# Sample retention states of a hybrid S5/retention step: vector multiply-adds with broadcast values in place of matmuls on split operands

## The chip, the cores and the metric

The kernel runs on one core of one Trainium2 chip. The metric is the device time of one execution in microseconds; lower is better. A core has five engines that run at the same time, each with its own instruction stream: TensorE (PE: matmuls and transposes, results in PSUM), VectorE (DVE), ScalarE (ACT), GpSimd (POOL) and SyncE (SP), whose queue here issues nearly all DMAs. On-chip data lies in SBUF, with 128 partitions, and in PSUM.

## The reference

One inference step of a single decoder layer, for a prompt of 256 positions and for 8 sample sequences of 8 positions each, 320 tokens together. RMS norm, one input projection to an S5 part and to q, k, v and gate of 8 retention heads of width 128, output projection, then a SwiGLU FFN (2048 to 5632 and back) and a last norm. The part that the change touches is the new retention state of the samples:

```python
gamma_h = 1 - 2 ** (-5 - h)                      # h = 0..7
# chunk of l = 8 positions for the samples, one state r0 (128 x 128) per head and sequence
k_decay = gamma_h ** (7 - t)                     # t = 0..7
r_new   = r0 * gamma_h ** 8 + einsum('md,me->de', k * k_decay[:, None], v)
```

So each of 64 states is the old one, scaled, plus eight outer products of a key with a value. The states are only an output; nothing later in the step reads them. Prompt states, attention outputs and the S5 part are as usual for such layers.

## The kernel before

All 320 tokens are columns of every matmul: columns 0 to 255 the prompt, 256 to 319 the samples (8 sequences b of 8 positions t). Every weight matrix is read once, in blocks of 128 x 1024 (512 KB, eight 128 x 128 tiles). To keep fp32 accuracy with the faster fp32r matmul, each operand is split in two parts: `wload` loads a block as `raw` (SP), ACT casts it to `hi` (L131), DVE subtracts to get `lo` (L133), and `gemm` runs three matmuls for each 128 x 128 tile: hi by hi, hi by lo, lo by hi (L143 to L145). In the first stages the pool `wp` holds three buffers each of raw, hi and lo; from the second FFN product on, a pool `wp2` with 4, 3 and 3 takes its place for weights, and `wp` is free for other use.

Stages in order of time: the input projection, one 128-wide column block after another (0 to 350 us of the span), and between its matmuls the S5 chunks and the retention heads; then output projection and GLU (350 to 485 us); then the FFN (to 1425 us), in four parts: `ffn_in(c)` makes 11 of 44 column pairs (gate, up), `ffn_out(c)` multiplies them by their part of the second matrix, in the order in 0, in 1, out 0, in 2, out 1, in 3, out 2, out 3.

What sets the order: PE and POOL run in the order in which the program traces them (a manual schedule). A small planner (`clk`, `spawn`, `run_due`) sums estimated matmul costs and resumes generators when their due time has come; so `head_k` runs 8.5 planned us after the k projection of its head, `head_v` 6.1 us after that of v. On DVE, ACT and SP a scheduler fixes the order at compile time from priorities; `wload` has a high one, so weights run ahead, and `tc.issue_after(x)` puts instructions behind x on x's engine.

The steps around the change:

- `do_k(h)`, after the k projection: `rot` makes the rotated keys `k_` (ACT, DVE), then POOL copies the sample columns to half of `ksp` (L883). `ksp` and `qsp` collect two heads.
- `head_k(h)`: PE transposes `k_` in three pieces into `pst` (L107), ACT scales two of them to `kd` for the prompt (L728) and the third to `kv[64:128, h]` (L729), the decayed keys of the samples by row. Then `pss`: scores of the prompt, and for odd heads `ksp` by `qsp`, the scores of two heads' samples. DVE multiplies by masks (`sm`, `smp`).
- `head_v(h)`: transposes of v, ACT scales them to `vT`, and copies the sample rows to `vsp` (L756) and to `kv[0:64, h]` (L757).
- The states, in `ffn_in(0)`: `states_split` splits `kv` into hi and lo and spreads both over partitions with 16 DMAs on ACT's queue; `states_load(h)` loads the eight old states of a head as `rt` (tag raw) and makes `vm`, the values masked per sequence (`bmk`); `states_add(h)` runs two matmuls of 512 columns into `psu` and two DVE instructions that scale the old states and add, then stores:

```python
ps = norm_ps("psu")
pe.matmul(ps, SU["k"][i][:, h], vm[:, q].rearrange("p b e -> p (b e)"), start=True, stop=True)
stt(rt[:, q], rt[:, q], float(GAM[h] ** NS), ps.rearrange("p (b e) -> p b e", e=P), MUL, ADD)
```

Of the kernel before, what the change touches and what calls it, by code (L numbers as in the profile page):

```python
# [12 lines left out]
F32 = mybir.dt.float32  # L13
F32R = mybir.dt.float32r
# [3 lines left out]
ADD, SUB, MUL = ALU.add, ALU.subtract, ALU.mult  # L18
PSUM = bass.MemoryType.PSUM

P = 128
D = 2048
KT = D // P
NP, NB, NS = 256, 8, 8
N = NP + NB * NS
H = 8
# [16 lines left out]

@with_exitstack
def hybrid_kernel(ctx, tc, xT, w_in, w_in4, w_out, w_glu, w_fi, w_fo, vecs, s5p, bc, x0,
                  r0, trig, masks, kdec, bmask, gq,
                  yT, s5p_o, s5s_o, rp_o, rs_o):
    nc = tc.nc
    pe, act, dve, pool, sp = nc.tensor, nc.scalar, nc.vector, nc.gpsimd, nc.sync
# [5 lines left out]
    def f(t):  # L55
        return t.bitcast(F32)
# [6 lines left out]
    mhalf = cst.tile([P, 4], F32, name="mhalf")  # L63
    pool.memset(mhalf, -0.5)
    vec = cst.tile([P, vecs.shape[1]], F32, name="vec")
    bmk = cst.tile([P, 4], F32, name="bmk")

    kv = cst.tile([P, H, P], F32, name="kv")
    voff = {}
    o = 0  # L70
    for nm, n in (("g_mix", 16), ("g_ffn", 16), ("g_fin", 16), ("d", 8), ("bglu", 8), ("gn", 8)):
# [33 lines left out]
    def tr(out, in_):  # L105
        m = in_.shape[0]
        pe.transpose(out, in_, ident[:m, :m])  # L107
        clk.now += 0.12
# [8 lines left out]


    wpool = [wp, (3, 3, 3)]
    last_hi = [None]  # L120

    def wload(src, nk, offset=3000):

        out = []
        with tc.high_priority(offset=offset):
            for k0 in range(0, nk, 8):
                m = min(8, nk - k0)
                raw, hi, lo = (wpool[0].tile([P, 8, P], d, name=n, tag=n, bufs=wpool[1][i])
                               for i, (n, d) in enumerate((("raw", F32), ("hi", F32R), ("lo", F32R))))
                sp.dma_start(raw[:, :m], src[:, k0:k0 + m])  # L130
                cast = act.copy(hi[:, :m], raw[:, :m])  # L131
                last_hi[0] = cast
                dve.tensor_tensor(lo[:, :m], raw[:, :m], f(hi[:, :m]), SUB)  # L133
                out += [(hi[:, i], lo[:, i]) for i in range(m)]
        return out

# [40 lines left out]
    def tt(out, a, b, op):  # L177
        dve.tensor_tensor(out, a, b, op)  # L178
        return out

    def stt(out, a, s, b, o1, o2):
        dve.scalar_tensor_tensor(out, a, s, b, o1, o2)
        return out
# [64 lines left out]
    rbc = mp.tile([P, N], F32, name="rbc")  # L248
    rtok = mp.tile([P, 3], F32, name="rtok")
    csr = mp.tile([P, 2, N], F32, name="csr")  # L250
    kdc = mp.tile([P, H, 3], F32, name="kdc")
    gqt = mp.tile([P, H, NS], F32, name="gqt")
    retp = mp.tile([P, H, N], F32, name="retp")

# [450 lines left out]
    def rot(ps, name):  # L705
        assert rot_t["ready"]
        with tc.high_priority(offset=EVAC):
            return rot_(ps, name)
# [11 lines left out]
    def head_k(h, q_, qg, k_, R):  # L720
        yield DL["k"]
        pst = misc("pst")
        for i, s in enumerate(STARTS):
            tr(pst[:, P * i:P * i + P], k_[:, s:s + P])
        kd = mp.tile([P, 2, P], F32, name="kd", tag="kd", bufs=1)
        with tc.high_priority(offset=EVAC):
            for i in range(2):
                act.mul(kd[:, i], pst[:, P * i:P * i + P], kdc[:, h, i:i + 1])  # L728
            act.mul(kv[64:128, h], pst[64:128, 2 * P:3 * P], kdc[64:128, h, 2:3])  # L729
        pss = misc("pss")  # L730
        mm(0.43, pss[:, 0:256], k_[:, 0:P], q_[:, 0:256], start=True, stop=True)
        mm(0.22, pss[:, 256:384], k_[:, P:256], q_[:, P:256], start=True, stop=True)
        if h % 2:
            mm(0.22, pss[:, 384:512], ksp, qsp, start=True, stop=True)
        sm = mp.tile([P, 384], F32, name="sm", tag="sm", bufs=1)
        mk = R["mk"]
        with tc.high_priority(offset=EVAC):
            tt(sm[:, 0:256], pss[:, 0:256], mk[:, 0:NP], MUL)
            last = dve.tensor_tensor(sm[:, 256:384], pss[:, 256:384], mk[:, 0:P], MUL)
            if h % 2:  # L740
                tt(smp, pss[:, 384:512], mk[:, NP:NP + P], MUL)
        if h == 0:
            with tc.issue_after(last.ins):
                s5_params3()
        R["kd"], R["sm"] = kd, sm

    def head_v(h, v_, qg, rt, R):
# [5 lines left out]
        with tc.high_priority(offset=EVAC):  # L753
            for i in range(3):
                act.mul(vT[:, i], pst2[:, P * i:P * i + P], rtok[:, i:i + 1])
        act.copy(vsp[64 * (h % 2):64 * (h % 2) + 64], vT[64:128, 2])  # L756
        last = act.copy(kv[0:64, h], vT[64:128, 2])  # L757
        if h == 0:
            rot_t["values"] = last
            with tc.issue_after(last.ins):  # L760
# [118 lines left out]
    def do_k(h, ps=None):  # L879
        ps = proj(9 + 4 * h) if ps is None else ps  # L880
        R = HS[h]
        k_ = rot(ps, "k_")
        pool.tensor_copy(ksp[:, 64 * (h % 2):64 * (h % 2) + 64], k_[:, NP:N])  # L883
        spawn(head_k(h, R["q_"], R["qg"], k_, R))
        run_due()
# [71 lines left out]
        k0 = k1  # L957
    ps0, ps1, pq, pk = accs
    for t_, s_ in ((x0t, x0), (csr, trig), (kdc, kdec),
                   (bmk, bmask), (gqt, gq)):  # L960
        sp.dma_start(t_, s_)
    for c in range(2):
        load_bc(c)
# [169 lines left out]
    def norm_ps(name):  # L1133
        return ps_n.tile([P, 512], F32, name=name, tag="n", bufs=2)
# [7 lines left out]

    SU = {}

    def states_split():
        kvh, kvl = (wp.tile([P, 8, P], F32R, name=n, tag=n, bufs=3) for n in ("hi", "lo"))
        act.copy(kvh, kv)
        tt(kvl, kv, f(kvh), SUB)  # L1150
        SU["k"] = [wp.tile([P, 8, P], F32R, name="hi", tag="hi", bufs=3) for _ in range(2)]
        SU["v"] = [wp.tile([P, 8, P], F32R, name="lo", tag="lo", bufs=3) for _ in range(2)]
        for i in range(2):
            for a in range(4):
                d = slice(32 * a, 32 * a + 32)
                act.dma_start(f(SU["k"][i][d]), f((kvh, kvl)[a // 2][64 + 32 * i:96 + 32 * i]))
                act.dma_start(f(SU["v"][i][d]), f((kvh, kvl)[a % 2][32 * i:32 * i + 32]))

    def states_load(h):
        rt = wp.tile([P, NB, P], F32, name="raw", tag="raw", bufs=3)  # L1160
        sp.dma_start(rt, r0[h])
        n = ("hi", "lo")[h % 2]
        vm = wp.tile([P, NB, P], F32R, name=n, tag=n, bufs=3)
        with tc.high_priority(offset=EVAC):
            for i in range(2):
                tt(vm[:, 4 * i:4 * i + 4], f(SU["v"][i][:, h]).unsqueeze(1).to_broadcast([P, 4, P]),
                   bmk.unsqueeze(2).to_broadcast([P, 4, P]), MUL)
        SU[h] = rt, vm

    def states_add(h):  # L1170
        rt, vm = SU.pop(h)
        for i in range(2):
            q = slice(4 * i, 4 * i + 4)
            ps = norm_ps("psu")
            pe.matmul(ps, SU["k"][i][:, h], vm[:, q].rearrange("p b e -> p (b e)"), start=True, stop=True)
            stt(rt[:, q], rt[:, q], float(GAM[h] ** NS), ps.rearrange("p (b e) -> p b e", e=P), MUL, ADD)
        sp.dma_start(rs_o[h], rt)

    def ffn_in(c):
        ahi = fp.tile([P, FCT, N], F32R, name="ahi", tag="ahi", bufs=2)  # L1180
        alo = fp.tile([P, FCT, N], F32R, name="alo", tag="alo", bufs=2)
        for i in range(FCT):
            n = c * FCT + i
            if n == 0:
                spawn(ffn_norm(), DL["n2"])
            pg = gemm("ps_fg", w_fi[2 * n], KT, hhi, hlo)
            g = fp.tile([P, N], F32, name="fg", tag="fg", bufs=2)
            tt(g, pg, rbc2, MUL)
            act.activation(g, g, AF.Silu)
            if n == 0:  # L1190
                wpool[:] = [wp2, WP2]
            pu = gemm("ps_fu", w_fi[2 * n + 1], KT, hhi, hlo)
            u = fp.tile([P, N], F32, name="fu", tag="fu", bufs=2)
            tt(u, pu, rbc2, MUL)
            tt(u, u, g, MUL)
            act.copy(ahi[:, i], u)
            tt(alo[:, i], u, f(ahi[:, i]), SUB)
            if c == 0:
                if i == 0:
                    states_split()  # L1200
                if 3 <= i:
                    states_add(i - 3)
                if 2 <= i < 2 + H:
                    states_load(i - 2)
        return ahi, alo

    wp2 = ctx.enter_context(tc.tile_pool(name="wp2", bufs=1, reuse_waits="tile"))
# [41 lines left out]
def _host(inp):  # L1249
# [58 lines left out]
    for h in range(1, H, 2):  # L1308
        pair[h, 0:64, 0:64], pair[h, 64:, 64:] = sm[h - 1], sm[h]
    A["masks"] = c(np.concatenate([mk, pair], 2).astype(f))  # L1310
    kd = np.zeros((P, H, 3))
    for i in range(2):
        kd[:, :, i] = gam[None, :] ** (NP - 1 - (P * i + np.arange(P)[:, None])) * sc
    kd[64:, :, 2] = gam[None, :] ** (NS - 1 - (tt_[:, None] % 8)) * sc
    A["kdec"] = kd.astype(f)
    A["bmask"] = c((np.arange(P)[:, None] // 8 % 4 == np.arange(4)[None, :]).astype(f))
    A["gq"] = c(np.broadcast_to((gam[:, None] ** (np.arange(NS) + 1.0))[None], (P, H, NS)).astype(f))
    return A

# [25 lines left out]
```

## Time and profile before

| | |
|---|---|
| median of 3 runs | 1439.0 us (1438.96 to 1439.07) |
| the profiled execution | 1438.91 us, span 1437.0 us |
| granted TensorE clock, mean | 0.998 |
| PE busy | 1421.6 us, 99% of the span |
| weight loads of PE | 1410.5 us, 98% |
| DVE busy | 846.1 us, 59% |
| ACT busy | 602.4 us, 42% |
| POOL busy | 101.1 us, 7% |
| DMA | 235.08 MB, mean 164 GB/s |

A matmul row such as "559.23 0.62 PE L1175 MATMUL psu<-lo,hi 128\*128 128x512 f32 x2" in the timeline has the start, the time from the first start to the last end, engine, line, operation, output and inputs by the program's names, shape and count. The end of a matmul is modelled, and matmuls overlap: what one costs is read from start to start. In lists of waits a row says who waited for whom: total us, times, longest.

### The profile page before, as it was taken

Reading aid. Unit: us, or ns where it says so; the run is one execution under the profiler, and the core shown is the slowest. Engines: PE = TensorE matmul, PEld = TensorE weight load, DVE = VectorE, ACT = ScalarE, POOL = GpSimd, SP = SyncE. Lnnn points to the kernel's source line nnn. Section 1 sums busy time; section 2 is a strip of 40 time slices with the busy share of each in tenths; the row PEclk is TensorE's granted clock in tenths of the full one; section 3 lists DMA queues with packets and bytes.
Section 4 is the critical chain, followed back from the end, with each engine's and each line's share of the span. In section 5 each row is a group of like instructions: output and inputs, shape, how many; then the busy total and the mean of one; then the engine's idle time right before and its main releaser. Section 6 shows DMA issues by size and latency. Waiting matters only on the chain.

```text
span 1437.0 us, 25722 instructions
## 1 busy us (share of the span) xinstructions
PE 1421.6 (99%) x10418; PEld 1410.5 (98%) x10418; DVE 846.1 (59%) x1374; ACT 602.4 (42%) x953; POOL 101.1 (7%) x177
## 2 busy tenths in 40 slices
PE   9999999999999999999999999999999999999997
PEld 8999999999999999999999999999999999999996
DVE  7988887777567655655444444444444444444554
ACT  7645555554355533333333333333333333333452
POOL 7530012210000000000000000000000000000001
PEclk9999999999999999999999999999999999999999
DMA  8555555556544666654444445444345444444442
GB/s 286 170 176 158 166 168 158 169 145 217 166 152 152 208 198 208 212 190 164 155 149 138 135 148 178 151 147 147 125 153 164 161 148 153 145 127 152 151 144 110
DMA packets 92774, 235.08 MB, mean 164 GB/s; under 512 B 26480, under 2 KB 40432, under 8 KB 92656
## 3 DMA queue, kind: packets, MB, share of 16 engines
q1 hardware_dynamic: 91744, 231.09, 49.5%
q10 hardware_dynamic: 912, 2.36, 0.6%
q8 instruction: 81, 1.33, 0.4%
q14 instruction: 37, 0.30, 0.1%
HBM read 220.66 MB, written 10.26 MB: 161 GB/s over the span
## 4 chain that ended last, share of the span: by engine, by line
PE 71%; DVE 0%; ACT 0%; DVEq 0%; issue 0%
PE ps_fg L143 7%; PE ps_fo L143 7%; PE ps_fo L145 7%; PE ps_fu L145 7%; PE ps_fg L145 7%; PE ps_fu L143 7%; PE ps_fu L144 7%; PE ps_fg L144 7%; PE ps_fo L144 7%; PE ps_o L143 1%; PE ps_o L144 1%; PE ps_o L145 1%; PE ps_g L144 1%; PE ps_g L145 1%; PE ps_g L143 1%; DVE x L178 0%
## 5 line engine op out<-in xcount | busy, mean ns | idle before, releaser
L133 DVE TENSOR_TENSOR lo<-raw,hi 128x1024 fp32r<-128x1024 f32 (+1 forms) x416 | 467.0, 1123 | 376.3 <-ACT hi L131 375.7
L131 ACT CAST hi<-raw 128x1024 fp32r<-128x1024 f32 (+1 forms) x416 | 401.8, 967 | 683.3 <-PE ps_fo L144 189.3
L143 PE MATMUL ps_fg<-hhi,hi 128*128 128x320 f32 x704 | 217.6, 309 | 0.0
L144 PE MATMUL ps_fo<-alo,hi 128*128 128x320 f32 x704 | 217.6, 309 | 0.0
L143 PE MATMUL ps_fo<-ahi,hi 128*128 128x320 f32 x704 | 217.6, 309 | 0.0
L145 PE MATMUL ps_fo<-ahi,lo 128*128 128x320 f32 x704 | 217.6, 309 | 0.0
L145 PE MATMUL ps_fg<-hhi,lo 128*128 128x320 f32 x704 | 217.4, 309 | 0.0
L145 PE MATMUL ps_fu<-hhi,lo 128*128 128x320 f32 x704 | 217.4, 309 | 0.0
L143 PE MATMUL ps_fu<-hhi,hi 128*128 128x320 f32 x704 | 217.4, 309 | 0.0
L144 PE MATMUL ps_fg<-hlo,hi 128*128 128x320 f32 x704 | 217.4, 309 | 0.0
L144 PE MATMUL ps_fu<-hlo,hi 128*128 128x320 f32 x704 | 217.4, 309 | 0.0
L143 PE MATMUL ps_p<-xhi,hi 128*128 128x320 f32 x560 | 177.5, 317 | 0.0
L145 PE MATMUL ps_p<-xhi,lo 128*128 128x320 f32 x560 | 173.1, 309 | 0.0
L144 PE MATMUL ps_p<-xlo,hi 128*128 128x320 f32 x560 | 172.9, 309 | 0.0
L144 PEld LDWEIGHTS ps_fg<-hlo,hi 128*128 128x128 f32 x704 | 132.4, 188 | 0.3
L143 PEld LDWEIGHTS ps_fg<-hhi,hi 128*128 128x128 f32 x704 | 132.3, 188 | 0.3
L143 PEld LDWEIGHTS ps_fu<-hhi,hi 128*128 128x128 f32 x704 | 132.4, 188 | 0.0
L144 PEld LDWEIGHTS ps_fu<-hlo,hi 128*128 128x128 f32 x704 | 132.4, 188 | 0.0
L145 PEld LDWEIGHTS ps_fu<-hhi,lo 128*128 128x128 f32 x704 | 132.4, 188 | 0.0
L145 PEld LDWEIGHTS ps_fg<-hhi,lo 128*128 128x128 f32 x704 | 132.3, 188 | 0.0
L143 PEld LDWEIGHTS ps_fo<-ahi,hi 128*128 128x128 f32 x704 | 132.2, 188 | 0.0
L144 PEld LDWEIGHTS ps_fo<-alo,hi 128*128 128x128 f32 x704 | 132.2, 188 | 0.0
(440 smaller groups left out, 1930.2 us busy)
## 6 DMA issues: line engine op xcount, KB each, us to landing
raw<-w_fi SPq DMA_DIRECT2D x176, 512.0 KB, 3.6
raw<-w_in SPq DMA_DIRECT2D x79, 512.0 KB, 4.0
raw<-w_fo SPq DMA_DIRECT2D x64, 512.0 KB, 3.5
raw<-w_out SPq DMA_DIRECT2D x32, 512.0 KB, 3.7
raw<-w_fo SPq DMA_DIRECT2D x64, 192.0 KB, 2.4
rt<-r SPq DMA_DIRECT2D x8, 512.0 KB, 5.1
raw<-w_glu SPq DMA_DIRECT2D x8, 512.0 KB, 3.4
raw<-r SPq DMA_DIRECT2D x8, 512.0 KB, 4.4
```

The lines of the kernel that those rows point to most:

```text
L131: cast = act.copy(hi[:, :m], raw[:, :m])
L133: dve.tensor_tensor(lo[:, :m], raw[:, :m], f(hi[:, :m]), SUB)
L143: pe.matmul(ps, hi, xhi[:, k], start=k == 0, stop=False)
L144: pe.matmul(ps, hi, xlo[:, k], start=False, stop=False)
L145: pe.matmul(ps, lo, xhi[:, k], start=False, stop=k == nk - 1)
```

## The change

The states of the samples are no longer made by matmuls. The decayed keys are kept in the layout that the projection gives (`kvf`: partition = key dimension, one scalar for each head, sequence and position), made by one POOL multiply in `do_k` in front of the copy to `ksp`. The third transpose of k and both `kv` writes on ACT go. The sample values of a head are stored from `vsp` to a DRAM tile `vd` by eight DMAs of 4 KB. In all four `ffn_in`, from n = 2 on, one or two steps follow each column pair, 70 in all. A step loads one position's values of one head for all sequences, the same row for all 128 partitions (128 x 1024, 512 KB, six buffers under the tags hi and lo of `wp`), for the first position also the old states, which POOL scales by gamma^8; three steps later DVE adds value times key for the eight sequences, eight instructions of 128 x 128, and three steps after the last position the states are stored. The steps' DMAs are put behind the weight load traced last, and their DVE instructions behind the `lo` traced last. `states_split`, `bmk` and the masks go.

```diff
+    kvf = cst.tile([P, H, NB, NS], F32, name="kvf")
+    drs = ctx.enter_context(tc.tile_pool(name="drs", bufs=1, space=bass.MemoryType.DRAM))
+    vd = drs.tile([H, NS, NB, P], F32, name="vd")
...
     def head_k(h, q_, qg, k_, R):
-        for i, s in enumerate(STARTS):
-            tr(pst[:, P * i:P * i + P], k_[:, s:s + P])
+        for i in range(2):
+            tr(pst[:, P * i:P * i + P], k_[:, P * i:P * i + P])
...
-            act.mul(kv[64:128, h], pst[64:128, 2 * P:3 * P], kdc[64:128, h, 2:3])
...
     def head_v(h, v_, qg, rt, R):
-        act.copy(vsp[64 * (h % 2):64 * (h % 2) + 64], vT[64:128, 2])
-        last = act.copy(kv[0:64, h], vT[64:128, 2])
+        r = 64 * (h % 2)
+        last = act.copy(vsp[r:r + 64], vT[64:128, 2])
+        for b in range(NB):
+            sp.dma_start(vd[h, :, b], vsp[r + NS * b:r + NS * b + NS])
...
     def do_k(h, ps=None):
         k_ = rot(ps, "k_")
+        pool.tensor_tensor(kvf[:, h], k_[:, NP:N].rearrange("p (b t) -> p b t", t=NS),
+                           kdt[:, h].unsqueeze(1).to_broadcast([P, NB, NS]), MUL)
         pool.tensor_copy(ksp[:, 64 * (h % 2):64 * (h % 2) + 64], k_[:, NP:N])
...
-    (states_split, states_load and states_add as told above)
+    SU = {"n": 0, "loads": []}
+    AHEAD = 3
+
+    def states_load(j):
+        h, t = divmod(j, NS)
+        if t == 0:
+            SU["rt"] = wp.tile([P, NB, P], F32, name="raw", tag="raw", bufs=3)
+            sp.dma_start(SU["rt"], r0[h])
+            pool.tensor_scalar(SU["rt"], SU["rt"], float(GAM[h] ** NS), None, MUL)
+        n = ("hi", "lo")[j % 2]
+        vb = wp.tile([P, NB, P], F32, name=n, tag=n, bufs=3)
+        sp.dma_start(vb, vd[h, t].unsqueeze(0).to_broadcast([P, NB, P]))
+        SU["loads"].append((h, t, vb, SU["rt"]))
+
+    def states_add():
+        h, t, vb, rt = SU["loads"].pop(0)
+        for b in range(NB):
+            stt(rt[:, b], vb[:, b], kvf[:, h, b, t:t + 1], rt[:, b], MUL, ADD)
+        SU[h] = rt
+
+    def states_step():
+        j = SU["n"]
+        SU["n"] += 1
+        with tc.issue_after(last_raw[0].ins), tc.issue_after(last_lo[0].ins):
+            if j < H * NS:
+                states_load(j)
+            if AHEAD <= j < H * NS + AHEAD:
+                states_add()
+            h, t = divmod(j - AHEAD - 3, NS)
+            if t == NS - 1 and h >= 0:
+                sp.dma_start(rs_o[h], SU.pop(h))
...
     def ffn_in(c):
-            if c == 0:
-                (states_split, states_add, states_load)
+            if n >= 2:
+                for _ in range(2 if n % 3 else 1):
+                    states_step()
```

More of the change, by code (lines that the diff above doesn't have):

```diff
@@ L45, in hybrid_kernel @@
 def hybrid_kernel(ctx, tc, xT, w_in, w_in4, w_out, w_glu, w_fi, w_fo, vecs, s5p, bc, x0,
-                  r0, trig, masks, kdec, bmask, gq,
+                  r0, trig, masks, kdec, kdf, gq,
                   yT, s5p_o, s5s_o, rp_o, rs_o):
@@ L65, in hybrid_kernel @@
     vec = cst.tile([P, vecs.shape[1]], F32, name="vec")
-    bmk = cst.tile([P, 4], F32, name="bmk")
-    kv = cst.tile([P, H, P], F32, name="kv")
+    kvf = cst.tile([P, H, NB, NS], F32, name="kvf")
+    drs = ctx.enter_context(tc.tile_pool(name="drs", bufs=1, space=bass.MemoryType.DRAM))
+    vd = drs.tile([H, NS, NB, P], F32, name="vd")
     voff = {}
@@ L119, in hybrid_kernel @@
     wpool = [wp, (3, 3, 3)]
-    last_hi = [None]
+    last_hi, last_raw, last_lo = [None], [None], [None]
     def wload(src, nk, offset=3000):
@@ L129, in wload @@
                                for i, (n, d) in enumerate((("raw", F32), ("hi", F32R), ("lo", F32R))))
-                sp.dma_start(raw[:, :m], src[:, k0:k0 + m])
+                last_raw[0] = sp.dma_start(raw[:, :m], src[:, k0:k0 + m])
                 cast = act.copy(hi[:, :m], raw[:, :m])
                 last_hi[0] = cast
-                dve.tensor_tensor(lo[:, :m], raw[:, :m], f(hi[:, :m]), SUB)
+                last_lo[0] = dve.tensor_tensor(lo[:, :m], raw[:, :m], f(hi[:, :m]), SUB)
                 out += [(hi[:, i], lo[:, i]) for i in range(m)]
@@ L250, in hybrid_kernel @@
     csr = mp.tile([P, 2, N], F32, name="csr")
-    kdc = mp.tile([P, H, 3], F32, name="kdc")
+    kdc = mp.tile([P, H, 2], F32, name="kdc")
+    kdt = mp.tile([P, H, NS], F32, name="kdt")
     gqt = mp.tile([P, H, NS], F32, name="gqt")
@@ L959, in hybrid_kernel @@
     for t_, s_ in ((x0t, x0), (csr, trig), (kdc, kdec),
-                   (bmk, bmask), (gqt, gq)):
+                   (kdt, kdf), (gqt, gq)):
         sp.dma_start(t_, s_)
@@ L1140, in ffn_norm @@
         act.copy(rbc2, next(rg))
[L1145 to L1177, printed above, removed]
+    SU = {"n": 0, "loads": []}
@@ L1197, in ffn_in @@
             tt(alo[:, i], u, f(ahi[:, i]), SUB)
-            if c == 0:
[L1199 to L1204, printed above, removed]
+            if n >= 2:
+                for _ in range(2 if n % 3 else 1):
+                    states_step()
         return ahi, alo
@@ L1310, in _host @@
     A["masks"] = c(np.concatenate([mk, pair], 2).astype(f))
-    kd = np.zeros((P, H, 3))
+    kd = np.zeros((P, H, 2))
     for i in range(2):
         kd[:, :, i] = gam[None, :] ** (NP - 1 - (P * i + np.arange(P)[:, None])) * sc
-    kd[64:, :, 2] = gam[None, :] ** (NS - 1 - (tt_[:, None] % 8)) * sc
     A["kdec"] = kd.astype(f)
-    A["bmask"] = c((np.arange(P)[:, None] // 8 % 4 == np.arange(4)[None, :]).astype(f))
+    A["kdf"] = c(np.broadcast_to((gam[:, None] ** (NS - 1.0 - np.arange(NS)) * sc)[None], (P, H, NS)).astype(f))
     A["gq"] = c(np.broadcast_to((gam[:, None] ** (np.arange(NS) + 1.0))[None], (P, H, NS)).astype(f))
```

## The prediction

> **What bounds the kernel now.** I read the page first (busy time per engine), then the busy time by stretches, then PE's own waits, then the timeline and single tiles around the places that the change touches.
>
> ```profile
> span 1437.0 us, 25722 instructions
> ...
> PE 1421.6 (99%) x10418; PEld 1410.5 (98%) x10418; DVE 846.1 (59%) x1374; ACT 602.4 (42%) x953; POOL 101.1 (7%) x177
> ```
> ```profile
> 900.00:1000.00 100.00, 100.00 (x684) 100.00 (x683) 47.67 (x57) 36.16 (x44) 0.00 (x0) 1.00 0.45 151
> ```
> ```profile
> PE pss L102 <- POOL ksp L883: 1.3, 1, 1.3
> ...
> PE pst L107 <- ACT kv L729: 0.4, 1, 0.4
> ```
>
> TensorE is the bound. In the FFN stretch (columns after its length: PE, PEld, DVE, ACT, POOL, granted clock, DMA share, GB/s) it starts 684 matmuls in 100 us, one per 0.146 us, at a granted clock of 1.00, while DVE works 47.7 us and POOL not at all. PE's list of waits is short, so matmuls that are taken out are gained one for one, and each new wait of PE is lost one for one. One old wait matters most: PE waited 1.3 us in `head_k` for `ksp`, a copy on POOL.
>
> The profiled run took 1438.91 us with a span of 1437.0 us, so 1.9 us lie around the span; the median of the runs is 1439.0, 0.1 above. I sum against the profiled run and shift by that 0.1.
>
> **Taken off PE: the state matmuls.** Timeline of PE:
>
> ```profile
> 559.23 0.62 PE L1175 MATMUL psu<-lo,hi 128*128 128x512 f32 x2
> 559.68 0.31 PE L143 MATMUL ps_fg<-hhi,hi 128*128 128x320 f32 x1
> ```
> ```profile
> 170.31 0.49 PE L107 MATMUL pst<-ident,k__2326 128*128 128x128 f32 x3
> 170.64 0.82 PE L102 MATMUL pss<-q__2189,k__2326 128*128 128x256 f32 x4
> 171.29 0.39 PE L102 MATMUL pss<-qsp,ksp 128*128 128x128 f32 x2
> ```
>
> Two `psu` matmuls push the next matmul from 559.23 to 559.68, 0.45 us. There are eight such pairs: 8 x 0.45 = 3.6 us. Three transposes of `pst` take 0.33 us, 0.11 each; one per head goes: 8 x 0.11 = 0.9 us. The ACT multiply that wrote `kv` goes too; it held PE for 0.4 us once (the wait above), of which the 0.36 us of that instruction less overlap, about 0.3 us, is gained, since the `kd` multiplies before it stay. Sum: 4.8 us (ends 4.5 and 5.2).
>
> **Added on POOL, in front of a copy that PE waits for.** In `do_k` the new multiply `kvf` comes before `ksp` in POOL's fixed order. Odd heads need `ksp` at once, for the last matmul of `pss`. The tile `ksp`, and PE's timeline at heads 1, 5 and 7 (head 3 stands above):
>
> ```profile
> L883 POOL COPY ksp<-k__1139 x1: 235/235/235, 85.3 to 85.3; 128x64 f32<-128x64 f32 x1
> ...
> L883 POOL COPY ksp<-k__2326 x1: 366/366/366, 165.5 to 165.5; 128x64 f32<-128x64 f32 x1
> ...
> L883 POOL COPY ksp<-k__3413 x1: 4990/4990/4990, 244.2 to 244.2; 128x64 f32<-128x64 f32 x1
> ...
> L883 POOL COPY ksp<-k__4288 x1: 3438/3438/3438, 307.8 to 307.8; 128x64 f32<-128x64 f32 x1
> ```
> ```profile
> 84.64 0.82 PE L102 MATMUL pss<-q__1056,k__1139 128*128 128x256 f32 x4
> 85.59 0.49 PE L102 MATMUL pss<-qsp,ksp 128*128 128x128 f32 x2
> ```
> ```profile
> 249.25 0.49 PE L102 MATMUL pss<-qsp,ksp 128*128 128x128 f32 x2 [1.33 <-POOL ksp L883]
> ```
> ```profile
> 310.95 0.82 PE L102 MATMUL pss<-q__4123,k__4288 128*128 128x256 f32 x4
> 311.61 0.39 PE L102 MATMUL pss<-qsp,ksp 128*128 128x128 f32 x2
> ```
>
> The same copy takes 0.235 us or 4.99 us. DVE's timeline over those stretches says why:
>
> ```profile
> 247.89 1.21 DVE L133 TENSOR_TENSOR lo<-raw,hi 128x1024 fp32r<-128x1024 f32 x1
> 249.02 0.47 DVE L178 TENSOR_TENSOR ev<-ev,py 128x320 f32<-128x320 f32 x1
> 249.78 0.42 DVE L178 TENSOR_TENSOR sm<-pss,mk 128x256 f32<-128x256 f32 x1 [0.28 <-PE pss L102]
> ```
> ```profile
> 311.12 0.51 DVE L182 SCALAR_TENSOR_TENSOR u<-y,y 128x320 f32<-128x320 f32 x1
> 311.55 0.75 DVE L178 TENSOR_TENSOR bl<-m,m 128x256 f32<-128x256 f32 x2
> 312.22 1.21 DVE L133 TENSOR_TENSOR lo<-raw,hi 128x1024 fp32r<-128x1024 f32 x1
> 313.35 1.28 DVE L178 TENSOR_TENSOR m<-raw_bc,lpc 128x512 f32<-128x512 f32 x2
> 314.67 0.42 DVE L178 TENSOR_TENSOR cl<-m,m 128x256 f32<-128x256 f32 x1
> 315.01 0.42 DVE L178 TENSOR_TENSOR sm<-pss,mk 128x256 f32<-128x256 f32 x1
> ```
>
> While DVE runs instructions with two SBUF inputs end to end, POOL stands. At head 5 it gets through at 249.1, when DVE comes to `ev<-ev,py` (one input in PSUM); at head 7 at 311.2, between two DVE instructions. A second POOL instruction needs a second such opening, or DVE's next instruction is in front of it:
>
> ```profile
> 97.42 0.31 POOL L790 TENSOR_SCALAR mv<-mv 128x3 f32<-128x3 f32 x1 [11.88 <-DVE mv L787]
> 97.80 0.66 POOL L791 TENSOR_SCALAR mv<-mv 128x3 f32<-128x3 f32 x1
> ```
> ```profile
> L507 POOL TENSOR_TENSOR e<-e,ecs 128x256 f32<-128x256 f32 x1 | 0.6, 639 | 0.0
> ...
> L511 POOL TENSOR_TENSOR e<-e,ecs 128x128 f32<-128x128 f32 x1 | 0.4, 432 | 0.0
> ```
>
> The second took 0.66 us where the first took 0.31. `kvf` itself (128x64, two inputs) I estimate at 0.33 us, by the line through 0.43 (128 wide) and 0.64 (256 wide). Head by head, with the DVE order of before:
> - Head 1: DVE is idle there; `ksp` ends 0.3 us later and PE already waits for it (0.95 us from `pss` to its last part, where head 3 has 0.65). Loss 0.3.
> - Head 3: `ksp` was ready over 5 us ahead of 171.29, so two openings fit. Loss 0.
> - Head 5: `kvf` goes in at 249.1; DVE then waits for `pss` anyway, so `ksp` follows at once. Loss 0.4; without that pause, up to 5.
> - Head 7: `kvf` takes the opening at 311.2, `bl`, `lo` and `m` follow end to end, the next opening is 314.65 (`cl` starts a moment late, as it needs `m`), `ksp` ends at 314.9. PE, which went on at 311.61, waits until then. Loss 3.3. It cannot be much more: at 315.0 DVE itself comes to `sm<-pss` and would stand. The other end is 0.2, if `ksp` slips in behind `kvf`.
>
> Sum of these losses: 4.0 us, ends 0.5 and about 9. I take 4.0, since heads 5 and 7 are read from their own rows. The even heads lose nothing: their `ksp` is used a head later. What is queued behind on POOL, the norm's chain, waits for DVE for 11.88 us (row 97.42).
>
> The Trainium skill, page "SBUF — State Buffer", section "Who interferes with whom", says that a DVE instruction with two SBUF inputs contends with a GpSimd instruction that reads SBUF, and that whoever issues first holds the shared ports for the whole instruction while the other blocks. The stalls here agree with the first half. Taken literally, though, `ksp` would wait for one DVE instruction, 1.2 us at most, where the row has 4.99; the measured row decides. By the page alone heads 3, 5 and 7 would lose nothing, and the sum would be 4.8 - 0.3 = 4.5 us gained.
>
> **Added on DVE and in the queues, during the FFN.**
>
> ```profile
> L133 DVE TENSOR_TENSOR lo<-raw,hi 128x1024 fp32r<-128x1024 f32 x352 | 431.3, 1226 | 270.3 <-ACT hi L131 269.7
> L131 ACT CAST hi<-raw 128x1024 fp32r<-128x1024 f32 x352 | 368.9, 1049 | 541.6 <-PE ps_fg L144 168.0 <-PE ps_fu L144 115.8 <-issue 78.9
> ...
> L182 DVE SCALAR_TENSOR_TENSOR hlo<-x,vec,hhi 128x320 fp32r<-128x320 f32 x16 | 8.6, 545 | 0.0
> ```
> ```profile
> L739 DVE TENSOR_TENSOR sm<-pss,mk x8: 269/280/282, 55.4 to 315.3; 128x128 f32<-128x128 f32 x8
> ```
> ```profile
> SPq L130 <- DVE lo L133: 972.6, 385, 7.5
> ```
> ```profile
> raw<-r SPq DMA_DIRECT2D x8, 512.0 KB, 4.4
> ```
> ```profile
> L593 SPq DMA_DIRECT2D kst<-via x64: 302/424/1572, 47.6 to 319.9; - x64
> ```
>
> 512 multiply-adds, 128x128, with a scalar from a tile: between 0.28 us (two inputs, that width) and 0.545 (such a scalar, 320 wide). I take 0.34, nearest the row of the same width, 0.27 from start to start as consecutive DVE rows overlap by some 0.08. That is 512 x 0.27 = 138 us over `ffn_in`'s 44 x 96 matmuls x 0.146 = 617 us: DVE goes from about 48% to 70%. What hides it: ACT casts a weight block the moment PE lets go of a buffer (the waits of `hi` on ps_fg and ps_fu), three buffers deep, so a `lo` block is finished 2 blocks x 24 matmuls x 0.146 = 7.0 us less 1.05 (hi) less 1.23 (lo) = 4.8 us before PE needs it. Two steps are 16 x 0.27 = 4.3 us: they fit even in one piece. Cost 0. POOL's new scaling of a 128x1024 tile, at most 0.64 + 768 x (0.639 - 0.432)/128 = 1.9 us by those rows, can hold DVE for as long, eight times: also inside 4.8 alone, and over it with two steps in one piece. Low end below nothing: the psu evacuations (16) and the split go from DVE; PE is never waiting for them.
>
> SP gets 64 loads of 512 KB with one source row for all partitions. The nearest row is the state load, same size, 4.4 us; a place for each: SP waits 972.6 us in total for `lo` to free buffers, so it has room. What is queued behind a load is the next weight block, wanted by ACT later than it lands. Cost 0; a load several times slower is the bad end. The 64 small stores of v (nearest: `kst`, 0.42 us of SP each) are 3.4 us of SP per head, behind which a weight block or a `kst` waits; the same 4.8 us of `lo` covers it. The eight stores of states, the loads `kdt` for `bmk`, and the ACT-queue copies that go cost PE nothing either way.
>
> **Sum.** 1438.9 - 4.8 + 4.0 = 1438.1, as a median 1438.2.
>
> **The rivals.**
> 1. *The openings come in time.* PE, DVE and ACT all shift by some tenths, and `ksp` may find its second opening early at head 7. Then 4.8 - 0.9 = 3.9 us are gained: 1435.1 (1434.2 if no head loses). For it: copies of 0.24 and 0.37 us at heads 1 and 3. Against: heads 5 and 7 above. The rule of the page, read literally, gives this rival's time, 1434.5.
> 2. *Slower by POOL.* `ksp` misses its opening at head 5 as well, DVE's next pause lying a full 5 us on (the 4.99 of the row). Losses 0.3 + 5 + 3.3 = 8.6: 1442.8. It decides from 7.7 us of losses on.
> 3. *Slower by the FFN.* DVE's scalings and two steps coincide, 4.3 + 1.9 = 6.2 against 4.8 us: 1.4 us once per head, 11 us: 1449. Or the one-row loads take some 12 us each, and weights come late: several us each, 64 times, over 1600. Against: 30% of DVE stays idle, and loads of that size landed in 4.4.
> 4. *PE gains nothing at all* is excluded: 16 matmuls and 8 transposes leave a full engine.
>
> **How the numbers follow.** A measurement of this kernel can tell about 0.2%, 2.9 us, from no change. Forecast (losses of 1.9 to 7.7): 0.50, its own range 1436.1 to 1441.8. Rival 1: 0.28, all faster. Rival 2: 0.09, rival 3: 0.13, slower. So faster 0.28, same 0.50, slower 0.22. The range goes from rival 1's end, 1434.2 less a little, to rival 2's 1442.8, and leaves out rival 3 and the worst of rival 2.
>
> **What would show it.** Right: no `psu`, two `pst` transposes for k per head; PE's list of waits with `pss <- POOL ksp` at 4 to 6 us in total, most at head 7; DVE near 70% in `ffn_in` with PE still at 684 matmuls per 100 us. Rival 1: that wait under 2 us. Wrong: PE waiting for `lo` or for a raw weight in the FFN, loads from `vd` landing well over 5 us, or PE waiting for `kst`, `toe` or `v` before 350 us because SP was late.

## The result, and the profile after

The changed kernel takes 1471.1 us (median of 5 runs, 1469.5 to 1471.4) against 1439.0: ratio 1.0222, 95% interval 1.0207 to 1.0237. It is 32 us slower, where 1438.2 was forecast. The profiled execution took 1469.48 us. In the experiments below, two runs of the kernel with one store took 1724.6 and 3589.7 us, far from its other six (1434.1 to 1436.0), and its ratio leaves them out.

The page of the changed kernel, its span and its engines:

```profile
span 1467.7 us, 26261 instructions
...
PE 1428.8 (97%) x10394; PEld 1416.6 (97%) x10394; DVE 958.6 (65%) x1853; ACT 598.0 (41%) x936; POOL 119.9 (8%) x193
```

PE has 24 matmuls fewer, as the change says, but its share fell from 99% to 97%. To find the place, the gate matmuls of the FFN, first and last start, before and then after:

```profile
L143 PE MATMUL ps_fg<-hhi,hi x704: 304/309/394, 486.7 to 1259.0; 128*128 128x320 f32 x176
```
```profile
L143 PE MATMUL ps_fg<-hhi,hi x704: 307/309/392, 520.8 to 1289.4; 128*128 128x320 f32 x176
```

The FFN starts 34.1 us later, and from its first to its last gate matmul it is 3.7 us shorter (768.6 against 772.3). So everything that the states do in the FFN went as hoped, and the loss lies wholly ahead of it, where the change adds only a multiply on POOL and 64 small stores on SP (and takes away a transpose and two ACT writes per head). PE's waits in the changed kernel, the top four rows:

```profile
PE py L102 <- DMA toe<-toe: 20.0, 7, 7.0
PE py L102 <- issue: 2.3, 1, 2.3
PE pb L102 <- DMA vd<-vsp: 1.6, 1, 1.6
PE pss L102 <- POOL ksp L887: 1.6, 1, 1.6
```

Seven times PE stands for `toe`, a small matrix of an S5 chunk that is shifted into place by DMAs on SP. No such wait was there before. The stretch of the projection, before and after (length, PE, PEld, DVE, ACT, POOL, clock, DMA share, GB/s):

```profile
40.00:400.00 360.00, 358.10 (x3203) 350.74 (x3202) 279.56 (x580) 188.65 (x400) 65.58 (x106) 1.00 0.54 168
```
```profile
40.00:400.00 360.00, 334.25 (x2961) 325.30 (x2960) 264.24 (x562) 172.33 (x369) 60.81 (x114) 0.96 0.49 155
```

PE stands 25.8 us of it instead of 1.9, and the clock granted is 0.96 instead of 1.00. The stops are 23.9 of the 34.1 us. Nearly all of the rest is the clock, which was granted at half in four stretches, each during or right behind the longer stops (columns as above):

```profile
214.02:220.84 6.82, 5.07 (x56) 4.93 (x57) 2.64 (x5) 2.14 (x5) 0.00 (x0) 0.50 0.62 211
255.00:265.20 10.20, 5.02 (x58) 4.54 (x59) 1.95 (x3) 1.04 (x5) 0.00 (x0) 0.50 0.48 132
340.31:343.72 3.41, 3.41 (x52) 3.19 (x51) 0.49 (x1) 0.42 (x1) 0.00 (x0) 0.50 0.53 190
371.04:381.26 10.22, 5.79 (x61) 5.43 (x62) 4.12 (x9) 2.38 (x5) 0.00 (x0) 0.50 0.74 244
```

PE was busy for 5.07 + 5.02 + 3.41 + 5.79 = 19.3 us of them, and half of that, 9.6 us, is lost. PE's timeline at the first of these stops:

```profile
211.79 0.36 PE L102 MATMUL py<-kst,toe 64*64 64x80 f32 x4
215.77 0.67 PE L102 MATMUL py<-kst,toe 64*64 64x80 f32 x10 [3.62 <-DMA toe<-toe]
...
218.00 0.47 PE L144 MATMUL ps_p<-xlo,hi 128*128 128x320 f32 x1
218.26 0.47 PE L145 MATMUL ps_p<-xhi,lo 128*128 128x320 f32 x1
218.53 0.47 PE L143 MATMUL ps_p<-xhi,hi 128*128 128x320 f32 x1
...
221.92 0.31 PE L144 MATMUL ps_p<-xlo,hi 128*128 128x320 f32 x1
```

After 3.62 us without work the projection's matmuls start every 0.267 us (218.00, 218.26, 218.53) instead of every 0.147, until the stretch ends at 220.8. PE's 5.07 us at half the clock cost some 2.5 us on top of the stop. The Trainium skill, page "TensorE: Matmul & The Clock Gate", section "What's actually happening", says that after at least one idle window of about 3.4 us the array runs at 1.2 instead of 2.4 GHz, until it has been busy for about as long. The trace agrees on the rate (320 columns at 1.2 GHz are 0.267 us, an estimate from that figure) and roughly on the length (PE was busy for 3.4 to 5.8 us of each stretch). It does not agree that 3.4 us without work are needed: the third stretch follows stops of 2.31 and 0.42 us, and in the kernel with the stores on ACT's queue (below) the one such stretch, 3.4 us long, follows a stop of 1.97 us. The measurement decides.

Why `toe` is late is seen on SP, which issues in a fixed order. SP's timeline for the same chunk, before; ACT had written the matrix at 189.84:

```profile
190.18 0.44 SPq L685 DMA_DIRECT2D yc<-back  x1
190.67 0.42 SPq L814 DMA_DIRECT2D rp_o<-rp  x1
191.19 4.34 SPq L651 DMA_DIRECT2D toe<-toe  x6
195.76 0.41 SPq L130 DMA_DIRECT2D raw<-w_in  x1
```

And after; ACT had written it at 192.07:

```profile
200.49 0.35 SPq L130 DMA_DIRECT2D raw<-w_in  x1
200.89 1.34 SPq L759 DMA_DIRECT2D vd<-vsp  x4
204.01 0.36 SPq L130 DMA_DIRECT2D raw<-w_in  x1
204.41 0.32 SPq L759 DMA_DIRECT2D vd<-vsp  x1
204.78 0.36 SPq L816 DMA_DIRECT2D rp_o<-rp  x1
205.24 1.89 SPq L652 DMA_DIRECT2D toe<-toe  x3
208.57 0.36 SPq L130 DMA_DIRECT2D raw<-w_in  x1
209.03 1.24 SPq L652 DMA_DIRECT2D toe<-toe  x2
211.31 0.34 SPq L130 DMA_DIRECT2D raw<-w_in  x1
211.70 0.60 SPq L652 DMA_DIRECT2D toe<-toe  x1
```

Before, the six shifts went out in one go from 191.19 on, and PE used them at 209.6. After, they start 14 us later, behind stores of `vd`, and in three pieces, each behind a weight load, to 212.3. Each weight load (`raw`) stands at the head of SP's order until DVE's `lo` frees a buffer; what is behind it stands as well, and between two of them only two to five small DMAs get out here. SP's largest wait in 100 to 350 us, before and then after:

```profile
SPq L130 <- DVE lo L133: 82.5, 42, 7.5
```
```profile
SPq L130 <- DVE lo L133: 76.5, 36, 6.4
```

SP has time left over, 76.5 us of waiting in 250. But the time lies in front of the weight loads, and the small copies cannot use it.

### The profile page after: what moved, and what is told of

The parts are those of the page before. It is cut to its first block, busy times and chain, and to the rows that moved or that the text cites. A ratio compares the mean times of both kernels' runs of the same rounds, so it can differ in the third digit from the quotient of the medians.

```text
span 1467.7 us, 26261 instructions
## 1 busy us (share of the span) xinstructions
PE 1428.8 (97%) x10394; PEld 1416.6 (97%) x10394; DVE 958.6 (65%) x1853; ACT 598.0 (41%) x936; POOL 119.9 (8%) x193
## 4 chain that ended last, share of the span: by engine, by line
PE 69%; DVE 0%; issue 0%; ACT 0%; DVEq 0%
PE ps_fu L144 7%; PE ps_fu L143 7%; PE ps_fo L143 7%; PE ps_fo L144 7%; PE ps_fo L145 7%; PE ps_fu L145 7%; PE ps_fg L143 7%; PE ps_fg L144 7%; PE ps_fg L145 7%; PE ps_o L145 1%; PE ps_o L143 1%; PE ps_o L144 1%; PE ps_g L144 1%; PE ps_g L145 1%; PE ps_g L143 1%; DVE x L178 0%
## 5 line engine op out<-in xcount | busy, mean ns | idle before, releaser
L145 PEld LDWEIGHTS ps_fo<-ahi,lo 128*128 128x128 f32 x704 | 132.4, 188 | 0.0
```

Of the source, the lines that this page charges most:

```text
L145: pe.matmul(ps, lo, xhi[:, k], start=False, stop=k == nk - 1)
```

## The experiments

Every kernel below was timed in turn with the kernel before (1439.2 to 1439.4 us there); "ratio" is to that, with its 95% interval. The theories: S, the 64 stores on SP's in-order queue make the S5 copies late; K, `kvf` on POOL makes `ksp` late for PE; and, for the FFN, whether DVE's new work costs nothing because it is hidden.

**The stores alone.** The kernel before with nothing but the 64 stores, which no one reads:

```diff
         last = act.copy(kv[0:64, h], vT[64:128, 2])
+        for b in range(NB):
+            sp.dma_start(vd[h, :, b], vsp[r + NS * b:r + NS * b + NS])
```

> The kernel before, with nothing changed but the 64 stores of sample values to DRAM added on SP's queue (nobody reads them). Theory S (the stores fill places of SP's in-order queue between waiting weight loads, so the toe copies of the S5 chunks come late and PE stands in front of them): nearly all of the loss in the projection stage appears here, 25 to 40 us over before, PE waiting for toe some 15 to 25 us. Rival K (POOL's extra multiply, or another order of the compiled schedule after the transposes and the ACT writes went, does it): under 5 us over before.

1469.6 us, ratio 1.0213 (1.0198 to 1.0228). The stores alone make 30 us of loss, against 32 for the whole change, and PE's longest waits are those for copies on SP:

```profile
PE py L104 <- DMA toe<-toe: 12.0, 5, 7.4
PE pb L104 <- DMA kst<-via: 4.4, 1, 4.4
PE pb L104 <- DMA yc<-back: 2.5, 1, 2.5
```

**Half of them**, `range(0, NB, 2)`, 32 stores:

> The kernel before plus four of the eight 4 KB stores per head on SP (32 in all, unread). Theory S, as a chain with slack: before, the toe copies were issued up to 15 us ahead of their matmuls, so half the queue places use up the slack and little more: between nothing and 12 us over before, far under half of the 30 us of eight stores. If the loss goes in proportion to the stores: 15 us over before.

1457.5 us, ratio 1.0124 (1.0110 to 1.0138): 18 us for 32 stores against 30 for 64. I had expected 12 us at most, as if there were slack to be used up first. On average a store costs about half a microsecond (0.56 and 0.47 us by the two runs). That is no price of each store, though: with 32 of them PE's stops for `toe` (13.7 us in all) lie at three places, at 244 to 250, 322 to 329 and 359 to 362 us, and before 240 us PE waits for no copy on SP at all. So there is slack at some chunks and none at others.

**The same stores on another queue.** The changed kernel with the 64 issues on ACT's queue:

```diff
-            sp.dma_start(vd[h, :, b], vsp[r + NS * b:r + NS * b + NS])
+            act.dma_start(vd[h, :, b], vsp[r + NS * b:r + NS * b + NS])
```

> The changed kernel with its 64 stores issued from ACT's queue instead of SP's. Theory S: the toe waits go, 1433 to 1440 us, unless ACT's own casts come late behind the issues. Rival K: it stays at 1465 to 1475.

1435.7 us, ratio 0.9978 (0.9969 to 0.9988): 35 us less for the same bytes, the same DMAs and the same arithmetic. PE's only wait for a copy on SP:

```profile
PE py L102 <- DMA toe<-toe: 0.7, 1, 0.7
```

So it is neither the traffic nor the DMA engines, but the place in SP's order. The Trainium skill, page "DMA: Bandwidth & Descriptors", section "Issuing engines are not separate DMA queues", says that issuing from several engines only saves the sequencer the time of initiating, usually small beside the DMA. Here the measurement differs and decides: the initiating itself is small (0.295 us a store by the row of `vd` below, 19 us in all, beside 76 us of waiting on that queue), and yet the move is worth 35 us, since an issue that waits for a buffer holds what is behind it.

**One store in place of eight**, still on SP, in a layout that one DMA can write (positions of a sequence together); the loads then gather eight pieces of 512 B for each partition:

```diff
-    vd = drs.tile([H, NS, NB, P], F32, name="vd")
+    vd = drs.tile([H, NB, NS, P], F32, name="vd")
...
-        for b in range(NB):
-            sp.dma_start(vd[h, :, b], vsp[r + NS * b:r + NS * b + NS])
+        sp.dma_start(vd[h].rearrange("b t p -> (b t) p"), vsp[r:r + 64])
...
-        sp.dma_start(vb, vd[h, t].unsqueeze(0).to_broadcast([P, NB, P]))
+        sp.dma_start(vb, vd[h, :, t].unsqueeze(0).to_broadcast([P, NB, P]))
```

> The changed kernel with one store of 32 KB per head in place of eight of 4 KB (the DRAM tile laid out by sequence, then position, so that each load takes eight pieces of 512 B per partition in place of 4 KB in one). Theory S, counted in queue places: 8 in place of 64, most of the loss goes, 1434 to 1445. If the bytes or the wait for the copy to vsp count, not the places: little goes, over 1460. If loads in 512 B pieces are slow, PE waits for lo or raw in the FFN instead.

1435.5 us, ratio 0.9973 (0.9962 to 0.9984). The tile `vd` in the changed kernel, then in this one, and this one's waits of PE for `toe`:

```profile
L759 SPq DMA_DIRECT2D vd<-vsp x64: 263/295/487, 56.7 to 355.0; - x64
```
```profile
L758 SPq DMA_DIRECT2D vd<-vsp x8: 499/504/551, 56.1 to 319.1; - x8
```
```profile
PE py L102 <- DMA toe<-toe: 0.8, 1, 0.8
```

Eight issues of 0.50 us in place of 64 of 0.295 are enough. The number of issues counts, not the bytes: those are the same. The layout of the loads changed with it, but they run in the FFN alone, behind the stage in question; what it does there is told at the end.

**`ksp` ahead of `kvf`**, rival K; the two POOL lines of `do_k` change places:

> The changed kernel with POOL's copy to ksp ahead of the kvf multiply. The prediction's own step: PE's waits for ksp (1.6 us) go, and if that delay sets off the later ones (rival K) the whole loss goes, to 1435 to 1445. Theory S: 1 to 3 us less than the changed kernel, 1468 to 1470.

1468.7 us, ratio 1.0207 (1.0191 to 1.0222). Its waits of PE, the first and a later row:

```profile
PE py L102 <- DMA toe<-toe: 20.9, 7, 7.0
...
PE pss L102 <- POOL ksp L885: 0.2, 1, 0.2
```

The wait for `ksp` falls from 1.6 to 0.2 us, and the time cannot be told apart from the changed kernel's. K is not the cause; it is worth a microsecond or two at most.

**Both mends** (one store, `ksp` first):

> The version that the runs so far point to: one store per head and the copy to ksp ahead of kvf. One store alone gave 1435.5, ksp first gave 2.4 us less than the changed kernel: 1433 to 1435.5, a gain of 0.25 to 0.4% on before. If the waits for ksp were already off the path once the toe copies come in time: the same as one store alone, 1435.5.

1434.7 us (1433.8 to 1436.9), ratio 0.9970 (0.9959 to 0.9980), the fastest median of all, but not to be told apart from one store alone. Its PE still waits 1.3 us for `ksp` at head 1, so the order on POOL settled nothing there.

**The S5 copies first.** The changed kernel, with the six `toe` shifts of a chunk put into the scheduler at high priority:

```diff
-        for u in range(2):
+        with tc.high_priority(offset=EVAC):
+            for u in range(2):
                 (the same shifts)
```

> The changed kernel, 64 stores on SP, with only the toe copies given a higher priority in the compiled order, so that they stand ahead of stores that are ready later or at the same time. Theory S by order in the queue: PE's waits for toe fall from 20 us to under 5 and the time to 1436 to 1452, the rest being kst and yc that still wait behind stores. If the number of queue places decides, whatever the order: over 1460.

1456.3 us, ratio 1.0120 (1.0106 to 1.0134): half of the loss goes, less than expected. PE no longer waits for `toe`, but for the copies that come next in the chunk:

```profile
PE pb L102 <- DMA kst<-via: 7.1, 2, 3.7
PE pb L102 <- DMA yc<-back: 5.6, 1, 5.6
```

The backlog stays and moves on to the next copy. `toe` was where it showed, not its cause.

**The stores late.** The changed kernel with four `vsp` tiles, kept for two heads each, and all 64 stores traced behind the last chunk:

```diff
-    vsp = mp.tile([P, P], F32, name="vsp")
+    vsps = [mp.tile([P, P], F32, name=f"vsp{i}") for i in range(4)]
...
     sp.dma_start(s5s_o, fins)
+    for h in range(H):
+        r = 64 * (h % 2)
+        for b in range(NB):
+            sp.dma_start(vd[h, :, b], vsps[h // 2][r + NS * b:r + NS * b + NS])
```

> The changed kernel with the same 64 stores of 4 KB on SP, traced after the last S5 chunk instead of in head_v (the sample values kept in four tiles until then). Theory S: place in time decides, no loss in the projection stage, 1433 to 1438. If 64 small stores cost by themselves (their issue or their traffic): over 1445.

1439.8 us, ratio 1.0004 (0.9995 to 1.0013): 31 us back, 4 to 5 short of the others and a little above the 1438 expected at most. The scheduler takes some of the stores ahead of their place in the text, four of them between the last chunk's copies at 310.7 us, and the last two `toe` waits are still there; that the one makes the other is not shown:

```profile
PE py L102 <- DMA toe<-toe: 4.4, 2, 3.5
```

**Unread stores at the lowest priority**, on the kernel before, with `tc.high_priority(offset=-2500)` around the store loop: the same question without the change's other parts.

> The kernel before plus the same 64 unread stores on SP, with a lowered priority, so that in the compiled order they stand behind every other copy that is ready. Theory S: the number of stores is the same, but the copies of the S5 chunks keep their places; the loss falls from 30 us to under 10. If 64 more issues on this queue cost wherever they stand between the weight loads: 20 us or more remain.

1454.1 us, ratio 1.0102 (1.0087 to 1.0117). A miss: no waits for `toe` or `kst` are left, but new ones have come:

```profile
PE po L104 <- ACT vT L757: 9.3, 1, 9.3
PE po L104 <- ACT vsp L759: 4.3, 1, 4.3
```

The late stores still read the single tile `vsp` when the head after next wants to write it; ACT stands, and PE behind it. **With four `vsp` tiles besides:**

> The kernel before plus the 64 unread stores on SP with lowered priority, and the sample values in four tiles in place of one, so that no later head's copy waits for a late store. With the lowered priority alone the waits for toe and kst were gone and 15 us were left, at PE waits for vT and vsp (13.6 us), which I put down to that reuse. If so: under 4 us over before. If stores on this queue cost by their number as well: 8 us or more over before.

1443.7 us, ratio 1.0032 (1.0020 to 1.0045). Those waits are gone, and of the 30 us for 64 stores on SP 4.4 are left, a little above what I had allowed, with two `toe` waits at the last chunk again:

```profile
PE py L104 <- DMA toe<-toe: 3.1, 2, 2.7
```

**The cover in the FFN.** The kernel with both mends, every multiply-add on DVE issued twice (so its states hold each product twice):

```diff
         for b in range(NB):
-            stt(rt[:, b], vb[:, b], kvf[:, h, b, t:t + 1], rt[:, b], MUL, ADD)
+            for _ in range(2):
+                stt(rt[:, b], vb[:, b], kvf[:, h, b, t:t + 1], rt[:, b], MUL, ADD)
```

> The version with one store and ksp first, with each of the 512 multiply-adds on DVE issued twice (so the sample states hold every product twice): 512 more of 0.34 us each. The prediction's cover in the FFN is 4.8 us between a finished lo block and PE's use of it; DVE would go from some 70% to over 90% there. If the cover holds for the order as compiled: no change, 1433 to 1436. If DVE now comes too late for lo: PE waits for lo in the FFN and the time rises by 10 to 100 us.

1454.9 us, ratio 1.0095 (1.0076 to 1.0114), 20 us above the kernel without the doubling. A stretch of the FFN and PE's waits:

```profile
700.00:800.00 100.00, 98.97 (x671) 98.15 (x670) 92.13 (x238) 33.70 (x42) 5.93 (x2) 1.00 0.76 224
```
```profile
PE ps_fg L143 <- ACT hi L131: 6.4, 3, 3.2
PE ps_fg L145 <- DVE lo L133: 2.2, 4, 0.7
```

DVE still has 8% left there, and yet PE waits, so it is not DVE's total that limits. Two doubled steps are 32 x 0.27 = 8.6 us in one piece, more than the 4.8 us that the prediction took for the lead of a weight block; the waits for `lo` fit that. But the larger part is for `hi`, and at the two longest of these stops (2.85 and 3.20 us, each with a stretch of 6.8 us at half the clock behind it) ACT itself waits for a weight from memory. The first:

```profile
688.07 1.04 ACT L131 CAST hi<-raw 128x1024 fp32r<-128x1024 f32 x1 [9.37 <-DMA raw<-w_fi]
```

So in this kernel the work is not free at twice the size, and at its own size it is; whether DVE or the weight loads gave out first is not shown.

## Why the prediction was wrong, point by point

- *"Taken off PE"*: right. `psu` 3.6 us forecast, 3.7 measured from first to last gate matmul. With the stores out of the way the kernel gains 3.5 to 4.7 us (1439.2 to 1435.7 and 1435.5, 1439.4 to 1434.7), against 4.8 forecast; PE still waits 0.7 to 2.0 us for `ksp` in these kernels, where it waited 1.3 before.
- *"Added on DVE and in the queues, during the FFN", cost 0*: right. The changed kernel there:

```profile
700.00:800.00 100.00, 100.00 (x684) 100.00 (x683) 70.48 (x148) 35.24 (x42) 2.77 (x1) 1.00 0.66 231
```
```profile
L182 DVE SCALAR_TENSOR_TENSOR raw<-hi,kvf,raw 128x128 f32<-128x128 f32 x256 | 71.5, 344 | 0.0
```

  684 matmuls in 100 us as before, DVE at 70% (forecast near 70%), 0.344 us for a multiply-add (taken: 0.34). POOL's scaling, put at 1.9 us at most, took 2.97, and held no one up that PE waited for: PE's list has no wait in the FFN. (The lead of a `lo` block, 7.0 less 1.05 less 1.23, is 4.7 us and not 4.8, and the upper end of the forecast's own range, 1439.0 - 4.8 + 7.7, is 1441.9; nothing hangs on either.)
- *"Added on POOL, in front of a copy that PE waits for", 4.0 us*: too high. Only head 1 waits, 1.6 us, where 0.3 was forecast; heads 5 and 7 lose nothing, and the old wait at head 5 is gone. At head 7 `kvf` took 0.43 us from 324.3 on and `ksp` 0.70 us from 324.7 on, one behind the other. The forecast had POOL wait there for an opening between DVE's instructions with two SBUF inputs. But DVE ran such instructions end to end here too (`xp<-v,v` from 324.16, `m<-raw_bc,gpc` from 324.61, `lo<-raw,hi` from 325.29 on). So the rule of the openings, read from two rows of before, does not hold as told, and what lets POOL in is not shown. For the time it is rival 1's case, and it was not what decided.
- *The step that failed*: "The 64 small stores of v (nearest: `kst`, 0.42 us of SP each) are 3.4 us of SP per head, behind which a weight block or a `kst` waits; the same 4.8 us of `lo` covers it", priced at 0. It cost 30 us by the run with the stores alone, and 35 to 36 us by the runs that take the stores off SP or make them few. The size of the issues was not the error (0.295 us each, less than taken). The cover was: the 4.8 us are the lead of a weight block, and they cover what stands ahead of a weight block. They do not cover `toe`, `kst` and `yc`, which stand on the same queue behind weight loads that wait for a buffer. The prediction named the sign ("PE waiting for `kst`, `toe` or `v` before 350 us because SP was late") and gave it no price and no rival of its own. The rows were to be had: SP's 972.6 us of waiting for `lo` was read as room, when it is where the queue is shut. The timeline of SP before shows it for one chunk: `toe` had only about 14 us from its last shift's issue (195.5) to PE (209.6), in which the next weight loads stand too.
- *Rivals*: none of the three on record happened as told in the changed kernel. The slower side was given 0.22, all of it to POOL and the FFN.

What stays open: how the 35 us divide between what a store takes itself and what stands behind weight loads because of it, and why the scheduler places so few small issues between two loads; its order is fixed at compile time and was only seen in the outcome. A fourth buffer for `raw` in the first stages, which might tell, was not tried.

## What to carry to other kernels

Count the issues that a change adds to an in-order queue, and ask who else has work on it, not how much time the queue has left: a DMA that waits for a buffer shuts the queue for all that comes behind. Where small transfers stand on the queue of the weight loads, make them one transfer or put them on another engine's queue; raising one copy's priority handed half of the delay to the next copy here. And a cover is the cover of one consumer: name for each added instruction every consumer behind it, and the lead of each.

## What the runs showed of the hardware that I had not expected

- PE paid for a stop of 3.6 us with some 2.5 us more at half the clock. Four such stretches cost 9.6 us, beside 23.9 us of stops, and a stop of 2.0 us was enough to set one off.
- A load of 512 KB whose source is the same 4 KB for all partitions, gathered in pieces of 512 B, landed a median of 11.8 us after its issue, the slow load feared in rival 3. It did come in the way of the weights: they landed after 8.3 us in place of 3.6 before, and ACT waited for them 120.7 us in place of 3.6. PE waited for none of it in the FFN. The changed kernel, which loads 4 KB in one piece for each partition, has no such wait in its list for ACT; its trace has no landing times for these loads. DMA issues of the kernel with both mends (count, KB each, median us to landing), and a wait of its ACT:

```profile
raw<-w_fi SPq DMA_DIRECT2D x176, 512.0 KB, 8.3
...
hi<-vd SPq DMA_DIRECT2D x32, 512.0 KB, 11.8
```
```profile
ACT hi L131 <- DMA raw<-w_fi: 120.7, 36, 7.2
```
